# Attention scores as rounded high/low products, with the latent-head preparation and the S5 readout placed between the neighbourhood heads

## The chip, the cores and the metric

The kernel runs on one core of a Trainium2 chip, in one launch. The metric is device time in microseconds (us); the median of three runs counts. PE is the matrix engine (TensorE), PEld its weight loads, DVE the vector engine, ACT the scalar engine, POOL the GpSimd engine, and SP the engine whose queue issues most transfers.

## What is computed

Two layers over 256 latent tokens and 256 context tokens of width 1024. Each layer is a half-step SwiGLU, a token mixer and a half-step SwiGLU. The mixer has one input projection, three kinds of heads and one output projection. In layer 1 the context rows are not needed at the end, so its context queries are left out. Cut to the mixer:

```python
def token_mixers(zx, zc, need_ctx_out, ...):
    qa, ka, va, cq, ckv, kr, u = split_cols(z)       # for x (latent) and c (context) tokens
    # neighbourhood attention: 6 heads of 64, 2-D window bias, plus all context keys
    a_x = na_attention(rms_norm(qa_x), rms_norm(ka_x), va_x, rms_norm(ka_c), va_c, na_rpb)
    # latent attention: 6 heads of 64 + 32 rotary
    kb, vb = mla_keys_values(ckv, kr, ...)           # rms_norm(ckv) @ w_ukv, rms_norm over 96
    qb = mla_queries(cq, ...)                        # rms_norm(cq) @ w_uq, rms_norm over 96
    b_x = blocked_joint_attention(rope_tail(qb_x), rope_tail(kb_x), vb_x, kb_c, vb_c)
    # S5: two linear scans, readout gelu(y) @ w_glu, a * sigmoid(g)
    s_x, s_c = s5_mixer(u_x, u_c, need_ctx_out, ...)
    ox = concatenate([a_x, b_x, s_x])
    if need_ctx_out:
        oc = concatenate([attend(qa_c, ka_c, va_c), attend(qb_c, kb_c, vb_c), s_c])
    return ox, oc

def attend(q, k, v, scale):
    p = softmax(einsum('bqhd,bkhd->bhqk', q, k) * scale)
    return einsum('bhqk,bkhd->bqhd', p, v)
```

## The kernel before

All work is written out by hand; each engine runs its instructions in the order of the code, and waits are set where tiles demand them. Activations are kept with tokens or with channels on the 128 partitions, 512 tokens together.

**Products.** Weights come through `take` in pieces: SP transfers a raw piece (three buffers), ACT rounds it to its high half (L251), DVE or POOL subtracts to get the low half (L252). `mm3` (L291 to L293) makes a dense product as high by high, high by low and low by high, three products of the rounded type F32R. `acc()` gives one of four PSUM banks, `tp()` one of four others (names t and b), used for transposes and small products. The attention scores are not made in this way: they are products of F32 operands, unrounded.

**The mixer** (`mixers`) runs in this order: projection of the column groups cq, ckv, qa, ka, va. Queries and keys of the neighbourhood heads are normalised by DVE (L1227) and transposed by PE (L1117, in `transp`) into `nqT` and `nkT`. The S5 scans run in the background of these groups. Then the columns zq and zk are transposed and split into `xn` (L1246), the S5 output into `yh` (L1254), the rotary table CG is made (L1266, L1270), twelve bias transfers are issued on SP (L1299), and the **latent-head preparation** runs: up-projection of queries (four token tiles in layer 0, two in layer 1) and keys (four), each in steps head, statistics, tail. The power of the statistics is on POOL (L1134), the scaling on DVE (L1327), the rotary part on POOL (L1283 to L1285). The values are copied by ACT (L1340). The S5 **readout** (GLU: sigmoid L1375, product, split L1384) and the transposes of the latent queries (`mqT`) follow.

**Attention** is a list of jobs, per pair of heads: two tiles of latent queries ("x") for each head, and in layer 0 one of context queries ("c") for each, 36 jobs in layer 0 and 24 in layer 1. A job has scores on PE (L1458 for "x", L1467 for "c"; for neighbourhood heads the bias is added as a product with a constant flip matrix, L1463), the maximum on DVE (L1470), the exponential on ACT (L1474), the reciprocal and the scaling on DVE (L1479, L1481), four transposes on PE (L1490), copies to PT (DVE L1493, ACT L1495 and L1498) and, for each pair, the product with the values (L1510) and its split (L1513, L1514). The scores run three jobs ahead of the transposes. POOL adds the window mask to the bias (L1429). The latent keys are transposed at job 4, the output projection's first piece is split at job 6. The output projection follows.

Of the kernel before, what the change touches and what calls it, by code (L numbers as in the profile page):

```python
# [93 lines left out]
class Net:  # L94
    def __init__(self, nc, tc, I, out, es):
# [24 lines left out]
        self.rho8 = [c.tile([128, 16], F32, name=f"rho8{l}") for l in range(2)]  # L120
        self.units = []
# [203 lines left out]
    def prologue(self):  # L325
        nc, I = self.nc, self.I
        self.norm_open()
        with lines(self.tc, name="pro", bufs=1) as pp:
# [11 lines left out]
            nc.vector.memset(self.cs, 0.0)  # L340
            nc.vector.memset(self.mh, -0.5)
# [834 lines left out]
    def mixers(self, l, pu, nxt):  # L1176
# [11 lines left out]
        nq = [mp.tile([128, 3, T], F32, name=f"n{x}T") for x in "qk"]  # L1188
# [5 lines left out]
        krs = lr.tile([128, 4], F32, name="krs")  # L1194
# [21 lines left out]
        for qi, name in enumerate(("qa", "ka")):  # L1216
            tiles = al if qi else qt_
            qn = np_.tile([128, 4, 384], F32, name="qn", bufs=2)
# [33 lines left out]
        for i in range(2):  # L1252
            S.activation(yh[:, 0, i, c], yT[:, i, c], AF.Copy)
            V.tensor_tensor(yh[:, 1, i, c], yT[:, i, c], yh[:, 0, i, c].bitcast(F32), op=OP.subtract)  # L1254
        esl.close()
        mp2 = pool(es, "mixb")
        bias = mp2.tile([128, 36, 64], F32, name="bias")
        rp = I["na_rpb"]
        mq = [mp2.tile([96, 6, T], F32, name=f"m{x}T") for x in "qk"]
        mv = mp2.tile([128, 4, 6, 64], F32, name="mv")  # L1260
        knp = pool(es, "kn")
        lp = pool(esl, "mla")
        CG = lp.tile([128, 2, 4, 32], F32, name="CG")
# [9 lines left out]
        def rope(x, t, i, nh):  # L1273
# [4 lines left out]
            tm = lp.tile([128, 6, 32], F32, name="tm", bufs=2)[:, 0:nh, :]  # L1278
# [7 lines left out]

        def upproj(ct, w, nk, n, t):
            ps = [self.acc(), self.acc()] if t % 2 else [self.tp(), self.tp()]
# [6 lines left out]
        w = self.take("uq", (l,))[:, :, 0:1728].rearrange("p s (k n) -> p s k n", k=3)  # L1295
        for hf in range(2):
            for hh in range(6):
                src = bass.AP(tensor=rp.tensor, offset=rp.offset + l * 2790 + (5 - hf) * 31 - 48 + 465 * hh, ap=[[1, 64], [31, 6], [1, 64]])
                nc.sync.dma_start(bias[64 * hf:64 * hf + 64, 6 * hh:6 * hh + 6, :], src)  # L1299
# [55 lines left out]
        for i, s_ in enumerate(seq):  # L1355
# [3 lines left out]
            if i == nqs + 0:  # L1359
                pass  # L1360
# [221 lines left out]
```

## Time and profile before

| | us |
|---|---|
| median of 3 runs | 1960.72 (1958.75 to 1962.05) |
| profiled execution | 1962.65 |
| its span, first to last instruction | 1960.7 |
| block of layer 0 (column transposes to first output projection product) | 118.74 |
| block of layer 1 | 93.60 |

The table is read from the profiled execution, except for the first line. The page gives each engine's busy time and the chain of work that ended last. Windows of the trace then show which engine is busy in a stretch and at what granted clock PE ran (1.00 is 2.4 GHz, 0.50 is 1.2 GHz). A wait is named by the instruction that waits and the one that released it. PE's matmuls are pipelined, so the price of one is the distance from its start to the next start, not its own length.

### The profile page before, as it was taken

To read this page: it belongs to the slowest core of one execution; us is meant where nothing else is said; L and a number is where in the kernel's file an instruction comes from. 1 tells how busy PE (TensorE), PEld (TensorE's weight loads), DVE (VectorE), ACT (ScalarE), POOL (GpSimd) and SP (SyncE) were. 2 spreads that over 40 slices of the span, in tenths; PEclk is the share of its full clock that TensorE was granted. 3 is DMA by queue.
4 is the path that set the end of the run, shared out by engine and by line. 5 is a ranking of instruction groups with operands and counts; after the bars stand their busy time and mean duration, and the time that the engine had idled before them with its cause. 6 is when DMAs were issued, how large, how long until landed. Compare 5 with 4: busy or idle time off the path is not lost.

```text
span 1960.7 us, 28001 instructions
## 1 busy us (share of the span) xinstructions
PE 1907.6 (97%) x11345; PEld 1557.8 (79%) x11345; DVE 907.3 (46%) x1596; ACT 678.8 (35%) x1128; POOL 574.3 (29%) x661
## 2 busy tenths in 40 slices
PE   7999999999999999999999999999999988999999
PEld 4777777788896587788888877777788878579999
DVE  6453233246457835232333554423433745655555
ACT  4421222224355634222212342122223435445343
POOL 2137461124535032100101314746212545231000
PEclk9999999999999999999999999999999999799999
DMA  9656566534431024533232455656523453036563
GB/s 309 178 166 200 174 205 212 165 97 141 132 105 51 2 86 130 173 117 96 88 105 76 139 158 167 201 160 217 178 75 113 141 166 100 22 126 215 175 194 108
DMA packets 364100, 277.75 MB, mean 142 GB/s; under 512 B 29854, under 2 KB 355812, under 8 KB 363972
## 3 DMA queue, kind: packets, MB, share of 16 engines
q1 hardware_dynamic: 361008, 268.44, 44.3%
q0 software_dynamic: 1888, 7.31, 1.0%
q8 instruction: 89, 1.46, 0.3%
q10 hardware_dynamic: 1076, 0.22, 0.1%
q14 instruction: 39, 0.32, 0.0%
HBM read 263.39 MB, written 12.55 MB: 141 GB/s over the span
## 4 chain that ended last, share of the span: by engine, by line
PE 84%; DVE 6%; POOL 4%; DMA 2%; ACT 1%; SPq 1%; issue 1%; POOLq 0%; ACTq 0%; DVEq 0%
PE acc L291 24%; PE acc L292 24%; PE acc L293 23%; PE b L467 3%; PE acc L1458 2%; PE t L1490 1%; DVE xm L562 1%; PE t L1510 1%; POOL ss L1134 1%; DVE xn L572 1%; PE acc L1463 1%; POOL sqs L523 1%; PE t L1100 1%; DMA bias<-in_na_rpb 1%; DVE xn L570 1%
## 5 line engine op out<-in xcount | busy, mean ns | idle before, releaser
L291 PE MATMUL acc<-xn,spl 128*128 128x512 f32 (+1 forms) x1664 | 598.0, 359 | 8.2 <-ACT mv L1340 5.9
L292 PE MATMUL acc<-xn,spl 128*128 128x512 f32 (+1 forms) x1664 | 590.7, 355 | 1.9 <-DVE xn L396 0.2
L293 PE MATMUL acc<-xn,spl 128*128 128x512 f32 (+1 forms) x1664 | 587.3, 353 | 0.1
L252 DVE TENSOR_TENSOR spl<-raw,spl 128x1024 fp32r<-128x1024 f32 (+2 forms) x312 | 390.2, 1287 | 276.0 <-ACT spl L251 273.8
L251 ACT ACTIVATE spl<-raw 128x1024 fp32r<-128x1024 f32 (+3 forms) x344 | 324.0, 990 | 303.9 <-PE acc L293 159.6
L291 PEld LDWEIGHTS acc<-xn,spl 128*128 128x128 f32 x1664 | 315.1, 189 | 71.7 <-issue 17.8
L292 PEld LDWEIGHTS acc<-xn,spl 128*128 128x128 f32 x1664 | 315.3, 189 | 46.7 <-DVE xn L570 4.3
L672 POOL TENSOR_TENSOR hid<-hv,hid 128x512 fp32r<-128x512 f32 (+1 forms) x88 | 101.8, 1156 | 852.2 <-ACT hid L671 852.2
L293 PEld LDWEIGHTS acc<-xn,spl 128*128 128x128 f32 x1664 | 315.3, 189 | 44.7 <-DVE spl L252 0.9
L291 PE MATMUL acc<-hid,spl 128*128 128x512 f32 (+1 forms) x740 | 265.2, 358 | 0.0
L292 PE MATMUL acc<-hid,spl 128*128 128x512 f32 (+1 forms) x740 | 262.0, 354 | 0.0
L293 PE MATMUL acc<-hid,spl 128*128 128x512 f32 (+1 forms) x740 | 261.7, 354 | 0.0
L669 DVE TENSOR_TENSOR hv<-sl,acc 128x512 f32<-128x512 f32 (+1 forms) x88 | 54.7, 621 | 365.1 <-PE acc L293 353.4
L671 ACT ACTIVATE hid<-hv 128x512 fp32r<-128x512 f32 (+1 forms) x88 | 50.9, 579 | 382.0 <-DVE hv L669 382.0
L729 DVE SCALAR_TENSOR_TENSOR h<-acc,mod,h 128x256 f32<-128x256 f32 x192 | 85.0, 479 | 210.8 <-PE acc L293 210.8
L291 PEld LDWEIGHTS acc<-hid,spl 128*128 128x128 f32 x740 | 139.8, 189 | 25.2 <-issue 6.4
L293 PEld LDWEIGHTS acc<-hid,spl 128*128 128x128 f32 x740 | 139.9, 189 | 19.7
L292 PEld LDWEIGHTS acc<-hid,spl 128*128 128x128 f32 x740 | 140.0, 189 | 18.5
L252 POOL TENSOR_TENSOR spl<-raw,spl 128x768 fp32r<-128x768 f32 (+3 forms) x32 | 65.3, 2041 | 211.4 <-ACT spl L251 199.5
L291 PE MATMUL acc<-spl,xn 128*128 128x384 f32 (+1 forms) x322 | 111.5, 346 | 0.0
L292 PE MATMUL acc<-spl,xn 128*128 128x384 f32 (+1 forms) x322 | 106.9, 332 | 0.4 <-POOL spl L252 0.3
L293 PE MATMUL acc<-spl,xn 128*128 128x384 f32 (+1 forms) x322 | 106.5, 331 | 0.0
(358 smaller groups left out, 1996.8 us busy)
## 6 DMA issues: line engine op xcount, KB each, us to landing
raw<-in_ffn_w_gu SPq DMA_DIRECT2D x176, 512.0 KB
raw<-in_w_mod SPq DMA_DIRECT2D x64, 1024.0 KB
raw<-in_ffn_w_down SPq DMA_DIRECT2D x32, 1024.0 KB
raw<-in_ffn_w_down SPq DMA_DIRECT2D x16, 768.0 KB
raw<-in_w_in SPq DMA_DIRECT2D x16, 768.0 KB
pmod<-in_w_mod SPq DMA_DIRECT2D x8, 1024.0 KB
raw<-in_w_out SPq DMA_DIRECT2D x8, 1024.0 KB
cld<-CL POOLq DMA_DIRECT2D x8, 576.0 KB, 4.8
```

The lines of the kernel that those rows point to most:

```text
L251: nc.scalar.activation(s[:, 0, a:b], raw[:, a:b], AF.Copy)
L252: (nc.gpsimd if mix and b == n else nc.vector).tensor_tensor(s[:, 1, a:b], raw[:, a:b], s[:, 0, a:b].bitcast(F32), op=OP.subtract)
L291: mm(out, sl[0], sr[0], start=start, stop=False)
L292: mm(out, sl[0], sr[1], start=False, stop=False)
L293: mm(out, sl[1], sr[0], start=False, stop=stop)
L467: nc.tensor.matmul(p[32 * j:32 * j + 32, 0:256], self.cs[:, k, 6 - 2 * w:38 - 2 * w], raw[:, k, :], start=(a == 0 and w == 0), stop=(a == ...
L523: nc.gpsimd.tensor_tensor(self.sq_sum[:, c], self.sq_sum[:, c], s[:, c], op=OP.add)
L669: nc.vector.tensor_tensor(hv[:, c], sl[:, c], pu[:, c], op=OP.mult)
L671: nc.scalar.activation(hd[:, 0, c], hv[:, c], AF.Copy)
L672: nc.gpsimd.tensor_tensor(hd[:, 1, c], hv[:, c], hd[:, 0, c].bitcast(F32), op=OP.subtract)
L729: self.nc.vector.scalar_tensor_tensor(self.h[:, n, c], ps[:, c], self.mod[l][:, gate, n, s:s + 1], self.h[:, n, c], op0=OP.mult, op1=OP.add)
L1458: mm(s, q[:, 256 + 128 * t:384 + 128 * t], k, start=True, stop=h >= 6)
```

## The change

Scores and bias are made of rounded products. Queries and keys are kept as a high and a low F32R half (`qz`, zero-padded to 128 rows so that a head's query meets a pair's keys, and `keyt`); a score is three products (L1522, context L1530), the bias two more (L1525) with its halves made on POOL (L1457, L1459, L1460). The transposes of `qa` and `ka` leave the groups; `keys` (per pair) and `queries` (per head) make them within attention, ACT the high half and DVE the low one. Latent-head preparation and readout become a generator, `latent()`, of which one piece runs after each job, so they lie among the neighbourhood heads. Latent heads are transposed by `latent_head`, one head each, two heads ahead. The scaling of the first "x" tile and of context tiles goes from DVE to POOL (L1544). The PT copy of odd context heads goes from ACT to DVE. Heads now run one after another and not in pairs of jobs. Bias transfers go out two heads at a time. The readout takes channel slots 0 and 1 and attention's outputs slots 2 to 7.

```diff
+        biases = [bias(h) for h in range(2)]
+        kr = mp.tile([128, 4, 32], F32, name="kr")
+        krs = mp.tile([128, 4], F32, name="krs")
...
-            def tr(j, qi=qi, tiles=tiles, qn=qn):
-                self.transp(nq[qi][:, j, 128 * tiles[0]:], lambda t: qn[:, t, 128 * j:128 * j + 128], 128, tiles, self.kg[l][:, 0:1] if qi else None)
-
-            self.q += [None, None, None] + [(lambda j=j, tr=tr: tr(j)) for j in range(3)]
...
-            ps = [self.acc(), self.acc()] if t % 2 else [self.tp(), self.tp()]
+            ps = [self.tp(), self.tp()]
...
+        def glu(n, wg):
+            pg = {}
+            for m in (2 + n, n):
+                pg[m] = self.tp()
+                for k in range(2):
+                    self.mm3(pg[m][:, c], (wg[:, 0, k, m * 128:m * 128 + 128], wg[:, 1, k, m * 128:m * 128 + 128]), (yh[:, 0, k, c], yh[:, 1, k, c]), k == 0, k == 1)
+            eg = mp2.tile([128, 576], F32, name="sq6")[:, 0:T]
+            S.activation(eg[:, c], pg[2 + n][:, c], AF.Sigmoid, bias=self.smT[l][:, 98 + n:99 + n])
+            V.scalar_tensor_tensor(eg[:, c], pg[n][:, c], self.smT[l][:, 96 + n:97 + n], eg[:, c], op0=OP.add, op1=OP.mult)
+            S.activation(xn[:, 0, n, c], eg[:, c], AF.Copy)
+            (V, P)[n].tensor_tensor(xn[:, 1, n, c], eg[:, c], xn[:, 0, n, c].bitcast(F32), op=OP.subtract)
+        def latent():
+            w = self.take("uq", (l,))[:, :, 0:1728].rearrange("p s (k n) -> p s k n", k=3)
+            for t in (2, 3, 0, 1):
+                rope(kr[:, t].unsqueeze(1), t, 1, 1)
+            seq = [(qhead, qstat, qtail, t) for t in [2, 3] + qt_[:-2]]
+            nqs = len(seq)
+            seq += [(khead, kstat, ktail, t) for t in al]
+            for i in range(len(seq) + 2):
+                if i == nqs:
+                    w = self.take("ukv", (l,), True)[:, :, 0:1536].rearrange("p s (k n) -> p s k n", k=2)
+                if i < len(seq):
+                    seq[i][0](seq[i][3], w)
+                for j in (1, 2):
+                    if 0 <= i - j < len(seq):
+                        seq[i - j][j](seq[i - j][3])
+                yield
+            wg = self.take("glu", (l,), False)[:, :, 0:1024].rearrange("p s (k n) -> p s k n", k=2)
+            for n in range(2):
+                glu(n, wg)
+                yield
+            self.ahead()
+        self.attention(l, need, qt_, qk, nv, qs, kn, mv, biases, bias, xn, mp2, latent())
...
+        def keys(p):
+            g = self.kg[l][:, 0:1]
+            kt = keyt[p % 2]
+            c = cols(lambda t: qk[1][:, t, 128 * p:128 * p + 128], al, 128)
+            S.activation(kt[:, 0], c, AF.Copy, scale=g)
+            V.scalar_tensor_tensor(kt[:, 1], c, g, kt[:, 0].bitcast(F32), op0=OP.mult, op1=OP.subtract)
+            for h in (2 * p, 2 * p + 1):
+                stacks[h] = [None, kt, None]
+        def queries(h):
+            r = slice(64 * (h % 2), 64 * (h % 2) + 64)
+            q = qz[h % 2]
+            c = cols(lambda t: qk[0][:, t, 128 * (h // 2):128 * (h // 2) + 128], qt_, 128)
+            S.activation(q[r, 0, t0:], c[r, 0:nq], AF.Copy)
+            V.tensor_tensor(q[r, 1, t0:], c[r, 0:nq], q[r, 0, t0:].bitcast(F32), op=OP.subtract)
+            b = biases.pop(0)
+            P.tensor_tensor(b, b, bc(self.k[:, K_WIN:K_WIN + 64].unsqueeze(1), [128, 6, 64]), op=OP.add)
+            bb = [ap.tile([128, 6, 64], F32R, name=f"bb{i}", bufs=2) for i in range(2)]
+            P.tensor_copy(bb[0], b)
+            P.tensor_tensor(bb[1], b, bb[0].bitcast(F32), op=OP.subtract)
+            if h < 4:
+                biases.append(bias(h + 2))
+            stacks[h][0] = q
...
+        def latent_head(h):
+            j, g = h - 6, self.kg[l][0:96, 1:2]
+            q, kt = qz[h % 2], keyt[1 - h % 2]
+            c = cols(lambda t: qs[t][:, j, :], qt_, 96)
+            S.activation(q[0:96, 0, t0:], c[0:96, 0:nq], AF.Copy)
+            V.tensor_tensor(q[0:96, 1, t0:], c[0:96, 0:nq], q[0:96, 0, t0:].bitcast(F32), op=OP.subtract)
+            c = cols(lambda t: kn[t][:, j, :], al, 96)
+            S.activation(kt[0:96, 0], c[0:96], AF.Copy, scale=g)
+            V.scalar_tensor_tensor(kt[0:96, 1], c[0:96], g, kt[0:96, 0].bitcast(F32), op0=OP.mult, op1=OP.subtract)
+            stacks[h] = q, kt, None
...
+        def after(i):
+            p, n = i // (2 * each), i % (2 * each)
+            if p < 2:
+                if n == 2 * each - 2:
+                    keys(p + 1)
+                    queries(2 * p + 2)
+                elif n == 2 * each - 1:
+                    queries(2 * p + 3)
+            elif p == 2:
+                if n == 2 * each - 2:
+                    for _ in latent:
+                        pass
+                    latent_head(6)
+                elif n == 2 * each - 1:
+                    latent_head(7)
+            elif n % each == each - 1 and i // each + 2 < 12:
+                latent_head(i // each + 2)
...
+            terms = [(q[r, i], ks[r, j]) for i, j in ((0, 0), (0, 1), (1, 0))]
+            if kind == "x":
+                for i, (q, k) in enumerate(terms):
+                    mm(s, q[:, 256 + 128 * t:384 + 128 * t], k, start=i == 0, stop=h >= 6 and i == 2)
                 if h < 6:
                     for i in range(2):
+                        mm(s[:, 256:512], self.flip, bb[i][:, 64 * (2 - 2 * t):64 * (6 - 2 * t)], start=False, stop=i == 1)
+                nb, n = 1, 512
...
+                for b in range(2):
+                    for i, (q, k) in enumerate(terms):
+                        mm(s[:, 256 * b:256 * b + 256], q[:, 128 * b:128 * b + 128], k[:, 0:256], start=i == 0, stop=i == 2)
...
+                (P if j[2] == 0 else V).tensor_scalar(e[:, i * n:i * n + n], e[:, i * n:i * n + n], su[:, i:i + 1], None, op0=OP.mult)
...
+            if t or (kind == "c" and h % 2):
+                V.tensor_copy(d, v)
+            else:
+                S.activation(d, v, AF.Copy)
...
+        for i in range(len(jobs) + LAG):
+            if i < len(jobs):
+                scores(jobs[i])
+                after(i)
+            if 0 < i <= len(jobs):
+                scale(jobs[i - 1])
+            if i >= LAG:
+                transposes(jobs[i - LAG])
+            for a in old.pop(0):
                 pv(*a)
+            old.append(pend[:])
+            pend.clear()
+            next(latent, None)
```

PE, layer 0, at the start of attention, before: after the column transposes (zq, zk) the first latent up-projection follows (t and b are PSUM banks, spl a weight piece).

```order
L1117 MATMUL t<-k,zq 128x128 x8
L1117 MATMUL b<-k,zq 128x128 x4
L1117 MATMUL t<-k,zk 128x128 x8
L291 MATMUL t<-spl,xn 128x288
L292 MATMUL t<-spl,xn 128x288
L293 MATMUL t<-spl,xn 128x288
L291 MATMUL t<-spl,xn 128x288
```

The same place of the changed kernel: transposes of a pair's keys (nk) and of two heads' queries (nq), the first score with its bias, then the first up-projection.

```order
L1119 MATMUL b<-k,zq 128x128 x4
L1119 MATMUL t<-k,zq 128x128 x8
L1119 MATMUL t<-k,zk 128x128 x4
L1119 MATMUL b<-k,zk 128x128 x4
L1436 MATMUL t<-k,nk 128x128 x4
L1436 MATMUL t<-k,nq 128x128 x8
L1522 MATMUL acc<-kt,qz_4762 128x512 x3
L1525 MATMUL acc<-bb_4781,flip 128x256
L1525 MATMUL acc<-bb_4782,flip 128x256
L292 MATMUL b<-spl,xn 128x288
```

So a score now stands between the transposes and the first up-projection.

POOL, layer 0, during the latent-head preparation, before: powers (L1134) and rotary parts (L1283 to L1285) of the latent queries (qn), with a window add (L1429).

```order
L1134 TENSOR_TENSOR ss_4886<-ss_4886,mh 128x6
L1134 TENSOR_TENSOR ss_4915<-ss_4915,mh 128x6
L1283 TENSOR_TENSOR tm<-qn,CG 128x6x8 x4
L1284 TENSOR_TENSOR qn<-qn,CG 128x6x32
L1285 TENSOR_TENSOR qn<-qn,tm 128x6x32
L1134 TENSOR_TENSOR ss_4952<-ss_4952,mh 128x6
L1283 TENSOR_TENSOR tm<-qn,CG 128x6x8 x4
L1284 TENSOR_TENSOR qn<-qn,CG 128x6x32
L1285 TENSOR_TENSOR qn<-qn,tm 128x6x32
L1134 TENSOR_TENSOR ss_4992<-ss_4992,mh 128x6
```

The same place of the changed kernel, with the scaling of tiles (L1544) and the bias splits (L1457 to L1460).

```order
L1544 TENSOR_SCALAR e<-e,su 128x512
L1136 TENSOR_TENSOR ss_4905<-ss_4905,mh 128x6
L1136 TENSOR_TENSOR ss_4949<-ss_4949,mh 128x6
L1290 TENSOR_TENSOR tm<-qs,CG 128x6x8 x4
L1291 TENSOR_TENSOR qs<-qs,CG 128x6x32
L1292 TENSOR_TENSOR qs<-qs,tm 128x6x32
L1544 TENSOR_SCALAR e<-e,su 128x256 x2
L1136 TENSOR_TENSOR ss_5007<-ss_5007,mh 128x6
L1290 TENSOR_TENSOR tm<-qs,CG 128x6x8 x4
L1291 TENSOR_TENSOR qs<-qs,CG 128x6x32
L1292 TENSOR_TENSOR qs<-qs,tm 128x6x32
L1457 TENSOR_TENSOR bias<-bias,k 128x384
```

Tile scalings and bias splits have come between the powers and the rotary parts, in one queue.

## Rows read from the trace of the kernel before

**Rows 1.** The profile page: shares of the chain that ended last, by engine

```profile
PE 84%; DVE 6%; POOL 4%; DMA 2%; ACT 1%; SPq 1%; issue 1%; POOLq 0%; ACTq 0%; DVEq 0%
```

**Rows 2.** Stretches: window, length, busy (count) by engine, granted clock, DMA share, GB/s

```profile
574.66:693.40 118.74, 112.89 (x621) 76.44 (x619) 92.60 (x214) 71.09 (x180) 33.91 (x45) 0.97 0.16 45
1639.60:1733.20 93.60, 86.22 (x427) 54.36 (x425) 67.35 (x150) 47.70 (x110) 29.33 (x43) 0.89 0.20 57
583.00:610.20 27.20, 23.79 (x129) 21.21 (x127) 19.72 (x47) 12.83 (x29) 24.71 (x38) 0.87 0.34 114
654.40:687.20 32.80, 32.80 (x190) 20.51 (x189) 28.07 (x72) 22.39 (x66) 0.00 (x0) 1.00 0.00 1
539.54:546.37 6.83, 6.31 (x21) 5.82 (x22) 2.23 (x3) 2.79 (x5) 1.87 (x1) 0.50 0.54 149
600.98:607.81 6.83, 5.80 (x15) 4.49 (x16) 4.60 (x12) 4.79 (x10) 5.28 (x6) 0.50 0.00 0
1665.94:1686.42 20.48, 19.55 (x38) 8.74 (x39) 10.83 (x26) 6.85 (x15) 8.95 (x11) 0.50 0.00 1
```

**Rows 3.** PE's waits by the window 505:693.4, then 1605:1733.2: total, times, longest

```profile
PE acc L291 <- ACT mv L1340: 3.4, 1, 3.4
PE t L1117 <- DVE qn L1227: 2.7, 1, 2.7
...
PE t L1117 <- DVE mqT L1125: 3.3, 1, 3.3
```

**Rows 4.** Timeline of PE in layer 0: start, length, operation, count

```profile
577.49 0.40 PE L291 MATMUL t<-spl,xn 128*128 128x288 f32 x1
...
638.17 1.13 PE L1467 MATMUL acc<-nkT,nqT 64*128 64x256 f32 x4
639.23 0.66 PE L1490 MATMUL t<-k,e 128*128 128x128 f32 x4
639.82 1.12 PE L1458 MATMUL acc<-nkT,nqT 64*128 64x512 f32 x2
640.87 0.70 PE L1463 MATMUL acc<-bias,k 128*128 128x256 f32 x2
641.41 0.60 PE L1490 MATMUL t<-k,e 128*128 128x128 f32 x4
...
665.03 0.60 PE L1490 MATMUL t<-k,e 128*128 128x128 f32 x4
665.47 1.02 PE L1458 MATMUL acc<-mkT,mqT 96*128 96x512 f32 x2
666.34 0.60 PE L1490 MATMUL t<-k,e 128*128 128x128 f32 x4
...
693.97 0.40 PE L293 MATMUL acc<-xn,spl 128*128 128x512 f32 x1
694.20 0.40 PE L291 MATMUL acc<-xn,spl 128*128 128x512 f32 x1
```

**Rows 5.** Groups by line on POOL, 505:693.4: count, busy us, mean ns, idle before

```profile
L1134 POOL TENSOR_TENSOR ss<-ss,mh 128x6 f32<-128x6 f32 (+1 forms) x17 | 22.7, 1338 | 19.6 <-DVE ss L1133 19.6
...
L1429 POOL TENSOR_TENSOR bias<-bias,k 128x384 f32<-128x384 f32 x6 | 5.3, 897 | 0.0
...
L1384 POOL TENSOR_TENSOR xn<-zq,xn 128x512 fp32r<-128x512 f32 x1 | 1.3, 1267 | 3.5 <-ACT xn L1383 3.5
```

**Rows 6.** Timelines of DVE and POOL, layer 0: start, length, operation, count

```profile
579.32 1.28 DVE L1254 TENSOR_TENSOR xn<-yT,xn 128x512 fp32r<-128x512 f32 x2
...
630.42 2.46 POOL L252 TENSOR_TENSOR spl<-raw,spl 128x1024 fp32r<-128x1024 f32 x1 [13.08 <-ACT spl L251]
...
631.36 1.81 DVE L1481 TENSOR_SCALAR e<-e,su 128x512 f32<-128x512 f32 x1
...
633.88 0.49 DVE L1481 TENSOR_SCALAR e<-e,su 128x512 f32<-128x512 f32 x1
```

**Rows 7.** Timeline of ACT at the layer-0 GLU

```profile
605.23 1.28 ACT L1375 ACT_TABLE_LOAD   x1
```

More of the change, by code (lines that the diff above doesn't have):

```diff
@@ L1217, in mixers @@
             tiles = al if qi else qt_
[L1218 removed]
+            qn = qk[qi]
             def norm(t, qn=qn):
@@ L1293, in upproj @@
             return ps
[L1295 to L1299, printed above, removed]
-        qs, kn = {}, {}
-        for t in (2, 3, 0, 1):
-            rope(zk[:, t, 256:288].unsqueeze(1), t, 1, 1)
-        new = lambda: lp.tile([128, 6, 96], F32, name="qn", bufs=4)
-        ss = {}
         def stat(key, sq, extra=None):
-            ss[key] = lp.tile([128, 6], F32, name="ss6", bufs=4)
+            ss[key] = mp2.tile([128, 6], F32, name="ss6", bufs=4)
             V.tensor_reduce(ss[key], sq, axis=AX, op=OP.add)
@@ new lines, in attention @@
+        keyt = [ap.tile([128, 2, T], F32R, name="kt"), ox[:, :, 7]]
+        qz = [ap.tile([128, 2, T], F32R, name=f"qz{i}") for i in range(2)]
+        for i in range(2):
+            r = slice(64 - 64 * i, 128 - 64 * i)
+            P.memset(qz[i][r].bitcast(F32), 0.0)
+        def after(i):
[15 more added lines that the diff above has]
+                latent_head(i // each + 2)
@@ new lines, in scale, with transposes @@
+        def scale(j):
+            e, su, nb, n = st[j]
+            V.reciprocal(su[:, 0:nb], su[:, 0:nb])
+            for i in range(nb):
+                (P if j[2] == 0 else V).tensor_scalar(e[:, i * n:i * n + n], e[:, i * n:i * n + n], su[:, i:i + 1], None, op0=OP.mult)
+        def transposes(j):
+            kind, h, t = j
+            e = st.pop(j)[0]
+            if (kind, h) not in PT:
+                PT[kind, h] = ap.tile([128, 4 if kind == "x" else 2, 256], F32, name=f"PT{kind}", bufs=3)
+            p = self.tp()
+            for i in range(4):
+                nc.tensor.transpose(p[:, 128 * i:128 * i + 128], e[:, 128 * i:128 * i + 128], self.ident)
+            if kind == "x":
+                d, v = PT[kind, h][:, :, 128 * t:128 * t + 128], p.rearrange("p (k q) -> p k q", k=4)
+            else:
+                d, v = PT[kind, h].rearrange("p k (t q) -> p t k q", t=2), p.rearrange("p (t k q) -> p t k q", t=2, k=2)
+            if t or (kind == "c" and h % 2):
+                V.tensor_copy(d, v)
+            else:
+                S.activation(d, v, AF.Copy)
+            if h % 2 and (t or kind == "c"):
+                pend.append((kind, h))
@@ new lines, in pv @@
+        def pv(kind, h):
+            o = self.tp()
+            nk = 4 if kind == "x" else 2
+            pts = [PT.pop((kind, h - 1)), PT.pop((kind, h))]
+            for k in range(nk):
+                for i in range(2):
+                    mm(o[64 * i:64 * i + 64, 0:256], value(h - 1 + i)(k), pts[i][:, k, :], start=(k == 0), stop=(k == nk - 1))
+            c = slice(256, 512) if kind == "x" else slice(0, 256)
+            f = h // 2 + 2
+            S.activation(ox[:, 0, f, c], o[:, 0:256], AF.Copy)
+            V.tensor_tensor(ox[:, 1, f, c], o[:, 0:256], ox[:, 0, f, c].bitcast(F32), op=OP.subtract)
@@ L1538, in run @@
+        for a in old[0] + old[1]:
+            pv(*a)
     def run(self):
```

226 lines of the change are left out of this document (69 added, 157 removed).

## The prediction

> **What bounds the kernel now.** I read the chain of waits first: 84% of the path to the end is matrix work on PE, 6% DVE, 4% POOL [rows 1]. So a change pays if PE gets less to do or waits less, and costs if another engine takes its place. The change touches one stretch in each layer, from the column transposes of the latent-rank inputs to the first output-projection product, and the column groups just ahead of it. The table by stretches [rows 2] gives for the layer-0 block 118.74 us with PE busy 112.89, DVE 92.60, ACT 71.09 and POOL 33.91, and for the layer-1 block 93.60 with PE 86.22. PE is the limit of both on average. It is not so everywhere: in the latent-head preparation (27.20 us) POOL is busy 24.71 and PE 23.79, while through the latent heads (32.80 us) PE is busy all the time and POOL does nothing. The same table shows three stretches in which PE's granted clock is 0.50, half of 2.4 GHz: 6.83, 6.83 and 20.48 us. Each comes right behind one of PE's longest waits, of 2.7, 3.4 and 3.3 us [rows 3]. A stretch at 0.50 does its PE work in twice the time, so it loses half of its busy PE time: 6.31/2 = 3.2 in the groups, 5.80/2 = 2.9 in the layer-0 block, 19.55/2 = 9.8 in the layer-1 block [rows 2].
>
> **Score products.** Prices are taken from start to start in the timeline of PE [rows 4]. A neighbourhood tile over the latent queries takes 640.87 − 639.82 = 1.05 for the score and 641.41 − 640.87 = .54 for the bias, 1.59 together; a context tile of the same heads 639.23 − 638.17 = 1.06; a latent tile 666.34 − 665.47 = .87. A rounded product of 512 columns, as the kernel uses everywhere else, takes 694.20 − 693.97 = .23, and I take half of it, .115, for 256 columns. Three of 512 are .69; with two bias products of 256 a neighbourhood tile comes to .92. A context tile, six products of 256, comes to .69. That these tiles keep this pace with their own weight loads is an estimate; its two ends are all of the gain below and none.
> Layer 0 has 12 neighbourhood tiles (12 × .67 = 8.0), 12 latent tiles (12 × .18 = 2.2), 6 context tiles of neighbourhood heads (6 × .37 = 2.2) and 6 of latent heads, for which I take the latent row's .87 (6 × .18 = 1.1): 13.5. Layer 1 has the first two: 10.2.
> The Trainium skill, page "FP8 and Floating Point Precision", section "TensorE Precision Notes", says that true FP32 takes four passes through the array. By it a tile of 512 columns takes 4 × .23 = .92; the latent row (.87) agrees, the neighbourhood row (1.05) does not, and the gain would be about 24 × .13 = 3 us smaller.
>
> **Transposes.** Four of them cost 665.47 − 665.03 = .44 [rows 4]. The groups lose six sets in layer 0 (2.6) and, with half the queries, the worth of 4.5 sets in layer 1 (2.0). Attention gains three sets for keys and six for queries, since a pair's query columns are now transposed for each head: 9 × .44 = 4.0, in layer 1 3 × .44 + 6 × .22 = 2.6. The latent heads keep their twelve sets and only take them later.
>
> **Groups.** With the transposes leaves their wait of 2.7 for the normalised queries, and with it, I expect, the half-speed stretch behind it (3.2): −2.6 − 2.7 − 3.2 = **−8.5** in layer 0. If another wait keeps the clock low the two last terms shrink; the least is −2.6. Layer 1 shows no such wait: **−2.0**.
>
> **Layer-0 block without new waits.** PE's busy time less the half-speed loss is 112.89 − 2.9 = 110.0; − 13.5 + 4.0 gives 100.5. To that come waits, which are the uncertain part.
> (a) The start. The first score now needs the low halves of keys and of two heads' queries, which DVE makes after the column work. DVE's two subtractions for the readout start at 579.32 and take 1.28 [rows 6], so it is free at 580.6; short products of table CG (an estimate, .3 if nothing disturbs them) and three subtractions at .64 each, half of those 1.28, end at 582.8. PE has done its transposes earlier: they now begin where the first up-projection product began, at 577.5 [rows 4], and three sets are 1.3, so 578.8. The wait is 4.0, between 2 and 6. It is as long as those that precede the three slow stretches, so I add the 2.9 that the slow stretch of this block loses now: 7.
> (b) The stretch in which preparation and neighbourhood heads share the engines, ten jobs. PE has about 33 there: the up-projections (4 × 18 products of 288 columns and 4 × 12 of 384, at .23 × columns / 512, are 17.6) and ten jobs at some 1.6 (a tile of .9, a set of transposes, and values now and then, which start late). POOL has its 24.71 [rows 2], less two window adds (L1429, .90 each [rows 5]), plus seven scaled tiles and two heads' bias splits. No row shows a scaling or a cast on POOL: between .5, DVE's price for the same tile [rows 6], and 1.27, POOL's own price for a subtraction of 512 [rows 5]; I take 1.15, nearer to POOL's row. A head's split is add, cast, subtract at .90, .75 and .90. So 24.7 − 1.8 + 8.1 + 5.1 = 36. POOL passes PE by 3, and its queue is in order: a scale waits behind a power (1.34 [rows 5]) that waits for DVE's sum, and behind the scale wait the transposes of that tile on PE; DVE's normalisation of the latent queries (L1327) in turn waits for the power. I take 8, between 3 and 20.
> (c) Pair boundaries, where the next pair's keys and queries are made one or two jobs ahead, and three more table loads on ACT for sigmoid and exponential between jobs, 1.28 each [rows 7]: 4, between 1 and 10. (d) The end: the last context tile's scaling is on POOL before its transposes: 2, between 0 and 4.
> 100.5 + 7 + 8 + 4 + 2 = 121.5 against 118.74: **+2.8**.
>
> **Layer-1 block.** 86.22 − 9.8 = 76.4; − 10.2 + 2.6 = 68.8. Waits: start 6.5, preparation 7 (jobs are fewer per head, so less PE work covers the same POOL chain), boundaries 3, end 1.5: 86.8 against 93.60: **−6.8**. The reason is the 20.48 us at half speed behind a wait for the first latent queries' transposes, which the new order spreads out.
>
> **Costed at nothing.** The bias transfers now stand in pairs in SP's queue and each waits until POOL has used the buffer two heads earlier; behind it stand weight transfers three units ahead, and the DMA engines are busy 0.16 to 0.20 in these blocks [rows 2]. The zeroing of the query buffers and a copy of the rotary columns on POOL lie where POOL is idle. Moving half the scales relieves DVE. If this cover were gone, a late weight piece would show as an output projection that waits, a few us.
>
> **Sum.** −8.5 + 2.8 − 2.0 − 6.8 = −14.5. The profiled execution took 1962.65, some 2 more than the median of 1960.72; the difference is applied to both: 1948.2 and **1946.2**.
>
> **Rivals.**
> 1. The waits are covered: in each block only the low ends remain, 6 in layer 0 (106.5, −12.2) and 5 in layer 1 (73.8, −19.8). With −10.5 in the groups −42.5, so 1918. For it: PE has work from two sources there, and the lag of three jobs between score and transposes is some 5 us at 1.6 a job. Against it: POOL's sum above PE's.
> 2. Slower: POOL and DVE stop each other. While POOL's split of 2.46 ran, DVE's scaling of 512 columns took 1.81 in place of .49 [rows 6]. Each layer moves 12 tiles or more to POOL and leaves 12 scalings on DVE, now beside a busy POOL even in the latent heads, where POOL was idle before. If all 24 that stay on DVE meet one and the path goes through them, 24 × 1.32 = 31.7; the time is 1946.2 + 31.7 = 1978. From 11 such meetings on the path the change no longer pays. Against it: the latent heads' DVE work falls, and a tile has three jobs before PE needs it.
> The Trainium skill, page "SBUF — State Buffer", section "Who interferes with whom", says that DVE and GpSimd share a port pair, that the first to issue holds it for the whole instruction, and that the other is blocked fully. It speaks against giving POOL the scales; the .49 that became 1.81 agrees.
> 3. The products do not run at the dense pace: no gain from them, +23.7, so 1970.
>
> **Chances.** Forecast .58 (1932 to 1958), rival 1 .18, rival 2 .19, rival 3 .05. The range reaches from just above the low rival to where half of the slow ones lie: 1920 to 1970. A measurement of this kernel can tell about 0.2% (4 us) from no change. Faster by more: .72, from rival 1 and most of the forecast; within: .09; slower: .19.
>
> **What would show it.** Right: tiles of score and bias at .9 in PE's timeline; no wait of PE in the query and key groups; a first score that waits for DVE's L1455; PE waits in the preparation that name POOL's L1544 or L1136; the layer-1 block about 7 shorter, the layer-0 block within a few us of its length. Wrong: scores that cost over 1.2 (rival 3); DVE scalings over 1 us in the latent heads and PE waiting for them (rival 2); preparation without PE waits (rival 1). The step on which most hangs is (b), and whether half speed follows the new waits.

## The result: slower by 2.3%, and the profile after

The changed kernel takes 2007.23 us (2004.01 to 2008.59, four runs) against 1961.38 before; the ratio is 1.0233, with a 95% interval of 1.0216 to 1.0251. The forecast was 1946.2 within 1920 to 1970, so sign and range are both missed.

The page of the changed kernel gives its span, busy time by engine and PE's granted clock in 40 slices:

```profile
span 2006.8 us, 28327 instructions
...
PE 1904.8 (95%) x11435; PEld 1582.0 (79%) x11435; DVE 914.7 (46%) x1585; ACT 689.8 (34%) x1146; POOL 656.2 (33%) x739
...
PEclk9999999999989899999999999999999988999999
```

PE's busy time is about what it was (1907.6 us before), while the span has grown by 46.1. By the start of the column transposes and of the first output-projection product in PE's timelines, the 46.1 lie so: 1.0 before the layer-0 block, 31.1 in it (149.83 against 118.74), 3.1 between the blocks, 10.9 in the layer-1 block (104.05 against 93.14, from the transposes' own start at 1640.04). After it the two kernels are equal to 0.1 us. The windows of these blocks, and of three stretches of the first, have the columns of [rows 2]:

```profile
575.65:725.48 149.83, 117.38 (x705) 93.50 (x703) 91.18 (x199) 79.84 (x192) 85.12 (x95) 0.89 0.15 38
1675.22:1779.28 104.06, 78.06 (x472) 61.62 (x470) 68.24 (x153) 56.99 (x128) 58.63 (x69) 0.93 0.22 54
583.00:630.00 47.00, 39.10 (x217) 35.78 (x219) 30.57 (x64) 21.82 (x55) 39.17 (x53) 0.85 0.36 82
630.00:672.00 42.00, 29.82 (x177) 22.02 (x174) 21.55 (x45) 23.95 (x49) 22.54 (x22) 0.88 0.12 41
672.00:719.00 47.00, 39.46 (x250) 29.85 (x249) 30.01 (x67) 26.42 (x73) 20.43 (x19) 0.89 0.00 1
```

Length less busy time is PE's idle time. In layer 0 it was 118.74 − 112.89 = 5.9 us and is 149.83 − 117.38 = 32.4; in layer 1 it was 7.4 and is 26.0. A mean clock of 0.89 means that some 2 × .11 × 149.83 = 33 us ran at half speed (7 before). Taking half of PE's busy time in such stretches off, read slice by slice from the windows, its work at full speed is 102.8 in layer 0 (110.0 before) and 71.7 in layer 1 (76.0). So PE has less to do, as intended, and the time is lost to waits and to the half speed that follows them: in layer 0 +26.6 idle, +11.6 half speed, −7.2 work; in layer 1 +18.6, −3.4 and −4.3.

PE's longest waits from the column groups to the end of the layer-0 block, in the columns of [rows 3], are not one wait but many:

```profile
PE t L1553 <- DVE e L1544: 7.3, 4, 2.6
PE t L1553 <- POOL e L1544: 6.6, 6, 2.9
PE acc L293 <- DVE spl L253: 6.0, 2, 3.7
PE b L1553 <- POOL e L1544: 3.6, 1, 3.6
PE t L1553 <- ACT PTc L1561: 3.0, 2, 2.3
PE t L292 <- DVE xn L1445: 2.9, 1, 2.9
PE acc L1522 <- ACT qz L1454: 2.6, 1, 2.6
PE t L292 <- DVE kt L1445: 2.5, 1, 2.5
```

L1553 are the transposes of the exponentials; they wait for the scaling (L1544) on DVE and on POOL and for copies of earlier tiles. L292 and t are an up-projection and a readout product that wait for the PSUM bank in which a key transpose still stands, until DVE has taken its low half (L1445). The wait of 6.0 for a weight piece is new too: it lies in the groups (3.7 and 2.2) and replaces the 2.7 of [rows 3].

One of the waits followed back, in the latent heads, in the timelines of DVE, ACT and PE (start, length, operation):

```profile
687.13 0.68 DVE L1533 TENSOR_REDUCE m<-acc 128x2 f32<-128x512 f32 x1
689.38 0.69 DVE L1472 TENSOR_TENSOR qz<-t,qz 96x512 fp32r<-96x512 f32 x1 [1.56 <-ACT qz L1471]
689.99 0.74 DVE L1475 SCALAR_TENSOR_TENSOR kt<-t,kg,kt 96x512 fp32r<-96x512 f32 x1
690.64 0.15 DVE L1542 RECIPROCAL su<-su 128x1 f32<-128x1 f32 x1
690.83 0.49 DVE L1544 TENSOR_SCALAR e<-e,su 128x512 f32<-128x512 f32 x1
```

```profile
687.85 0.47 ACT L1537 ACTIVATE e<-acc,m 128x256 f32<-128x256 f32 x1 [1.09 <-DVE m L1533]
...
688.76 0.58 ACT L1471 ACTIVATE qz<-t 96x512 fp32r<-96x512 f32 x1
```

```profile
688.30 0.94 PE L1522 MATMUL acc<-xn,qz 96*128 96x512 f32 x3
691.47 0.30 PE L1553 MATMUL t<-k,e 128*128 128x128 f32 x1 [2.22 <-DVE e L1544]
```

DVE has taken the maximum of a context tile by 687.8. Its next instruction in the queue is the low half of a later head's queries, which needs ACT's high half, and that stands on ACT behind the two exponentials of the same context tile. DVE idles 1.56, makes two low halves, and only then scales a tile of an earlier job, for which PE waits 2.22 us in all. DVE's 1.56 return at each of the later latent heads; PE waits behind every second of them: 1.96, 2.22 and 2.57.

### The profile page after: what moved, and what is told of

It is laid out like the page before. It is cut to its first block, busy times and chain, and to the rows that moved or that the text cites. A ratio compares the mean times of both kernels' runs of the same rounds, so it can differ in the third digit from the quotient of the medians.

```text
span 2006.8 us, 28327 instructions
## 1 busy us (share of the span) xinstructions
PE 1904.8 (95%) x11435; PEld 1582.0 (79%) x11435; DVE 914.7 (46%) x1585; ACT 689.8 (34%) x1146; POOL 656.2 (33%) x739
## 5 line engine op out<-in xcount | busy, mean ns | idle before, releaser
L292 PE MATMUL acc<-xn,spl 128*128 128x512 f32 (+1 forms) x1648 | 591.3, 359 | 2.3 <-DVE xn L571 1.2
L293 PE MATMUL acc<-xn,spl 128*128 128x512 f32 (+1 forms) x1648 | 584.6, 355 | 1.9 <-DVE xn L398 0.2
L294 PE MATMUL acc<-xn,spl 128*128 128x512 f32 (+1 forms) x1648 | 580.9, 353 | 0.2 <-DVE spl L253 0.2
L253 DVE TENSOR_TENSOR spl<-raw,spl 128x1024 fp32r<-128x1024 f32 (+2 forms) x312 | 398.2, 1313 | 278.6 <-ACT spl L252 276.8
L292 PEld LDWEIGHTS acc<-xn,spl 128*128 128x128 f32 x1648 | 311.7, 189 | 64.2 <-issue 17.8
L293 PEld LDWEIGHTS acc<-xn,spl 128*128 128x128 f32 x1648 | 311.8, 189 | 46.9 <-DVE xn L572 4.6
L294 PEld LDWEIGHTS acc<-xn,spl 128*128 128x128 f32 x1648 | 311.7, 189 | 44.1 <-DVE spl L253 0.9
L292 PE MATMUL acc<-hid,spl 128*128 128x512 f32 (+1 forms) x740 | 265.2, 358 | 0.0
L292 PEld LDWEIGHTS acc<-hid,spl 128*128 128x128 f32 x740 | 139.8, 189 | 25.2 <-issue 6.4
L293 PEld LDWEIGHTS acc<-hid,spl 128*128 128x128 f32 x740 | 140.0, 189 | 18.6
L293 PE MATMUL acc<-spl,xn 128*128 128x384 f32 (+1 forms) x288 | 98.0, 340 | 8.5 <-DVE spl L253 8.2
L292 PE MATMUL acc<-spl,xn 128*128 128x384 f32 (+1 forms) x288 | 101.2, 351 | 0.0
L294 PE MATMUL acc<-spl,xn 128*128 128x384 f32 (+1 forms) x288 | 97.5, 338 | 0.0
L669 ACT ACTIVATE sl<-acc 128x512 f32<-128x512 f32 (+1 forms) x88 | 47.7, 541 | 133.8 <-PE acc L294 127.5
```

The lines of the kernel that those rows point to most:

```text
L253: (nc.gpsimd if mix and b == n else nc.vector).tensor_tensor(s[:, 1, a:b], raw[:, a:b], s[:, 0, a:b].bitcast(F32), op=OP.subtract)
L292: mm(out, sl[0], sr[0], start=start, stop=False)
L293: mm(out, sl[0], sr[1], start=False, stop=False)
L294: mm(out, sl[1], sr[0], start=False, stop=stop)
L669: nc.scalar.activation(sl[:, c], pg[:, c], AF.Silu)
```

## The experiments

All ratios are to the kernel before, timed in the same series.

**Order and place of the scaling.** Run 1 moves the scaling ahead of the preparation of later heads:

```diff
             if i < len(jobs):
                 scores(jobs[i])
-                after(i)
             if 0 < i <= len(jobs):
                 scale(jobs[i - 1])
+            if i < len(jobs):
+                after(i)
```

> One thing is reordered against the changed kernel: in each job the scaling of the job before (reciprocal, multiply) is written ahead of the preparation of a later head's keys and queries, not behind it. Theory A (the low halves of later keys and queries wait on DVE for ACT behind the job's own exponential, and hold up the scaling behind them): the waits of PE's transposes for the DVE-scaled tile (7.3 us in layer 0, 3.7 to 4.1 us waits in layer 1) go and with them the half-speed stretches that follow; about 18 us less, 1989. Theory B (the tiles are late because POOL takes 1.56 to 1.83 us for a scaling): 0 to 4 us less, 2003 to 2007.

Measured: 1999.71, ratio 1.0194 (1.0174 to 1.0214), some 7.5 us less than the change, between the two theories. The waits for DVE-scaled tiles went (7.3 to .6), but those for POOL-scaled ones stayed:

```profile
PE t L1553 <- POOL e L1544: 9.0, 11, 3.0
PE b L1553 <- POOL e L1544: 3.6, 1, 3.6
```

Run 2 puts all scalings on DVE:

```diff
-                (P if j[2] == 0 else V).tensor_scalar(e[:, i * n:i * n + n], ...)
+                V.tensor_scalar(e[:, i * n:i * n + n], ...)
```

> All scalings on DVE, as in the kernel before; nothing else is changed. Theory A: the queue order stays, the DVE queue only gets longer; 0 to 6 us less, 2001 to 2007. Theory B: PE's waits for POOL-scaled tiles (10.0 and 6.8 us) go, with some half-speed time; about 18 us less, 1989. If POOL and DVE had stopped each other at the shared port, more still.

Measured: 2009.96, 1.0251 (1.0234 to 1.0268): no gain. PE's waits only changed their name:

```profile
PE t L1553 <- DVE e L1544: 9.4, 6, 2.3
...
PE b L1553 <- DVE e L1544: 2.9, 1, 2.9
```

Run 3 has both edits.

> Scaling first and all of it on DVE. If A and B both hold and add up: about 35 us less, 1972. If either alone is the cause, no better than the better of the two single runs, about 1989.

Measured: 1999.17, 1.0189 (1.0170 to 1.0208), as run 1. Theory B has fallen: POOL's long scalings are not the cause, though PE waits by that name. Theory A holds for a sixth of the loss.

Run 4 runs the preparation whole ahead of attention (`for _ in latent: pass` ahead of `keys(0)`).

> The latent-head preparation and the readout run whole ahead of attention, as in the kernel before; scores, scalings and order of the attention jobs stay those of the changed kernel. Theory C (the loss lies in the interleaving, POOL's and ACT's queues shared by two kinds of work): about 15 us less, 1992. Theories A and B: the waits of the jobs stay and the preparation has no cover, 0 to 8 us more, 2007 to 2015.

Measured: 2004.70, 1.0224 (1.0202 to 1.0245), not to be told from the change. As a net account, putting it in pieces neither costs nor gains as long as the rest stands, and theory C falls. Under that net lie two sums: waits behind the pieces go (they are followed back in the next section), and PE idles 42.09 − 30.05 = 12.0 us ahead of the first score, in a preparation that nothing covers:

```profile
575.77:617.86 42.09, 30.05 (x178) 25.96 (x176) 31.84 (x66) 22.30 (x45) 28.23 (x41) 0.92 0.08 26
```

PE's idle time in the whole layer-0 block (length less busy time) hardly moves through these four runs: 30.3, 28.7, 30.1 and 30.1 us, against 32.4 in the change.

**Depth, low halves, banks, products.** These four stand on top of run 1. Run 5 has one job more between a score and its transposes:

```diff
-        LAG = 3
+        LAG = 4
```

> On top of scaling first: scores run four jobs ahead of the transposes instead of three (one more buffer of e, m and su; one PTc buffer less to make room). Theory F (the distance between score and transposes is too short now that a score takes PE .7 to .9 us and the way over DVE, ACT and POOL is longer): PE's waits for scaled tiles, 12.6 us in layer 0 and some 10 in layer 1, go mostly, with half-speed time behind them: about 18 us less than 1999.7, 1982. Theory G (the PSUM banks of the column transposes are held by the chain ACT high half, DVE low half, and all else in the same ring waits): 0 to 3 us less, 1997 to 2000.

Measured: 1993.12, 1.0168 (1.0150 to 1.0186), 5 to 7 us less than run 1: between the two theories.

Run 6 leaves the low halves of queries and keys out:

```diff
-            V.tensor_tensor(q[r, 1, t0:], c[r, 0:nq], q[r, 0, t0:].bitcast(F32), op=OP.subtract)
...
-            terms = [(q[r, i], ks[r, j]) for i, j in ((0, 0), (0, 1), (1, 0))]
+            terms = [(q[r, 0], ks[r, 0]) for _ in range(3)]
```

> On top of scaling first: the low halves of queries and keys are not made (DVE's subtractions are left out) and the products read the high half in their place, so that PE's work is the same; the result is not the attention's. Theory G: the waits for banks held by the subtractions go (about 13 us in layer 0, as much in both layers with the half-speed time): about 20 us less, 1980. Theory F: DVE has 24 x .7 = 17 us less to do in layer 0, but the way of a tile is the same: 0 to 5 us less, 1995 to 2000.

Measured: 1986.16, 1.0122 (1.0106 to 1.0138), 14 us less than run 1 with the same products on PE, between the theories and nearer to G. The waits for L1445 are gone from the list. Run 6 takes away three things at once: the time of the subtractions on DVE, their place in its queue, and their hold on a bank that others wait for.

Run 7 gives the column transposes another ring of banks (`self.acc()` for `self.tp()` in `cols`).

> On top of scaling first: the column transposes of queries and keys in attention take their PSUM bank from the ring of the scores instead of the ring shared by the other transposes, the value products and the up-projections. Theory G, if the shared ring is the point: waits of L292, L1553 and L1571 for DVE's subtractions go, about 10 to 15 us less, 1985 to 1990. Theory F: the same or, since scores now wait for those banks, up to 5 us more, 1999 to 2005.

Measured: 1995.65, 1.0180 (1.0156 to 1.0204), 4 us below run 1 but within its interval: no clear gain, which speaks against the bank as the larger part of the 14. Run 3 has 14 us more on DVE in the layer-0 block than run 1 (105.43 busy against 91.24) and takes the same time, which speaks against DVE's time as such. That leaves the place of the low halves in DVE's queue; this is argued and not shown by a run of its own.

Run 8 keeps the order but goes back to one F32 product per tile, and so makes no low halves and no bias splits either:

```diff
-            terms = [(q[r, i], ks[r, j]) for i, j in ((0, 0), (0, 1), (1, 0))]
+            terms = [(q[r, 0].bitcast(F32), ks[r, 0].bitcast(F32))]
...
-                        mm(s[:, 256:512], self.flip, bb[i][:, 64 * (2 - 2 * t):64 * (6 - 2 * t)], ...)
+                    mm(s[:, 256:512], self.k[:, K_FLIP:K_FLIP + 128], bb[0][...], start=False, stop=True)
```

> On top of scaling first: the new order with the old products: one F32 product per score tile and one for the bias, no low halves and no bias split (the operands are rounded high halves read as F32, so the result is that of rounded operands). PE's work rises by about 20 to 24 us over both layers, DVE's and POOL's falls. If the new products and their halves are what costs, it falls towards the kernel before plus the extra transposes, about 1970. If the new order alone costs (preparation in pieces, heads one after another), it stays at 1995 to 2005.

Measured: 1980.61, 1.0096 (1.0081 to 1.0111). With more work on PE it is 19 us faster than run 1, and still 19 slower than before, between the two expectations. Along this path the 46 us are 7.5 for the place of the scaling, 19 for the rounded products with their halves and bias splits, and 19 for the order. Its two blocks, columns as in [rows 2]:

```profile
573.43:709.73 136.30, 116.65 (x657) 83.42 (x656) 78.39 (x178) 79.67 (x192) 75.96 (x83) 0.95 0.16 41
1659.36:1752.34 92.98, 79.80 (x447) 55.99 (x445) 55.87 (x132) 56.97 (x128) 49.32 (x57) 0.96 0.24 60
```

The layer-1 block is as long as before; the layer-0 block is 17.6 longer. Its idle time is 136.30 − 116.65 = 19.7 against 5.9 before, which is 13.8 of the 17.6.

**What is left of the order, with F32 products.** Run 10 takes run 8 and the preparation ahead, run 11 takes run 8 and scalings on DVE, run 13 both, run 14 both and LAG 4.

> The run with F32 scores in the new order, with the latent-head preparation and readout whole ahead of attention, as in the kernel before. If the 17.5 us that this order still costs in layer 0 come from preparation in pieces: about 15 us less, 1966. If they come from the order of jobs and the column transposes within attention: 1980 or, the preparation being uncovered, up to 10 us more.

> The run with F32 scores in the new order, with all scalings on DVE, which has no low halves to make there. If the waits for POOL-scaled tiles (9.6 us in layer 0) are what is left: about 12 us less with the half-speed time, 1969. If those waits only pass to another step of the tile's way: 1978 to 1982.

> F32 scores in the new order, with both the preparation ahead of attention and all scalings on DVE. Left of the change are the order of jobs, head by head, and the column transposes within attention. If the two shares add up: 1980.6 - 3.9 - 5.2 = 1971.5, and what is left (10 us) is the price of job order and transposes. If each only showed a part of the same wait and the two together free it: 1962 to 1966.

> The same with scores four jobs ahead. If what is left is the distance between a score and its transposes (heads one after another bring the context tile, which needs two exponentials and two scalings, into every third place): 5 to 8 us less, 1964 to 1966. If it is the transposes and their copies in the queues: 1970 to 1972.

Measured: 1976.69, 1.0072 (1.0058 to 1.0085); 1975.41, 1.0069 (1.0056 to 1.0083); 1973.84, 1.0065 (1.0050 to 1.0080); 1971.21, 1.0045 (1.0029 to 1.0062). Each alone gives some 4 to 5 us, with an interval that still meets that of run 8, and both together hardly more (6), so the two do not add up in full. With LAG 4 (six runs, 1966.76 to 1974.96), 10 of the 19 us are gone and 9 remain. In run 13 the longest waits of PE are at the head of attention (L1436 are the column transposes, L1516 the first score, L1453 ACT's copy of its queries, L1360 and L1361 the readout, whose banks the transposes wait for):

```profile
PE t L1436 <- ACT sq L1360: 3.7, 2, 2.7
PE acc L1516 <- ACT qz L1453: 3.3, 1, 3.3
PE t L1436 <- DVE sq L1361: 1.6, 1, 1.6
```

Its window up to just before the first score (620.92), in the columns of [rows 2]:

```profile
578.85:620.00 41.15, 30.17 (x177) 26.10 (x175) 30.97 (x65) 21.39 (x43) 27.30 (x41) 0.93 0.08 26
```

PE idles 11.9 us up to that score and 1.5 in the rest of the block; the kernel before idles 5.9 in all of it. So in layer 0 what is left lies in the uncovered preparation and between it and the first score, and not in the order of the jobs behind it. What the up-projections lose by their smaller ring of banks (`ps` in the diff) was not tried by itself.

**All mends with the rounded products.** Run 12 has run 1, LAG 4 and the other banks; run 15 adds preparation ahead and scaling on DVE.

> The changed kernel with three mends together: scaling first, four jobs of distance, column transposes in the banks of the scores. Alone they gave 7.5, 6.6 and 4.1 us. If they are separate waits: about 1989. If they are the same waits under other names: 1991 to 1993, as the best of them.

> The changed kernel, rounded products, with all mends at once: preparation ahead of attention, scaling first and on DVE, four jobs of distance, columns in the banks of the scores. If the products and low halves cost by DVE's time, which is now the fullest beside PE: 1985 to 1990, no better than three mends. If the mends add up: about 1978.

Measured: 1989.80, 1.0143 (1.0127 to 1.0158), and 1993.77, 1.0166 (1.0149 to 1.0183), the second above both of its expectations. No arrangement tried with low halves comes within 1.4% of the kernel before.

**A part of the change that pays.** Run 8 showed something else: an F32 score of a neighbourhood head took .86 us and not 1.05, and its zero-padded queries have 128 rows where the kernel before multiplies 64. Run 9 puts only this into the kernel before (the other rows are zeroed once by POOL, and one PTc buffer less makes room):

```diff
-                    return nq[0][r, h // 2, :], nq[1][r, h // 2, :], ...
+                    return qz[h % 2], nq[1][:, h // 2, :], ...
...
+            def pad(h):
+                r = slice(64 * (h % 2), 64 * (h % 2) + 64)
+                P.tensor_copy(qz[h % 2][r, t0:], nq[0][r, h // 2, t0:])
```

> The kernel before with one thing of the change: the neighbourhood heads' queries are copied by POOL, two heads ahead, into two buffers of 128 rows whose other 64 rows are zero, so that F32 score products run over 128 rows instead of 64. If the 1.05 us of a score before came from the 64-row operands (the F32 run in the new order showed .86, and .43 for the bias instead of .54): 12 x .2 + 6 x .2 + 12 x .1 = 4.8 us less in layer 0, 3.6 in layer 1, 1953. If the price comes from elsewhere, or POOL's copies hold up DVE's scalings: 1960 to 1965.

Measured: 1957.11, 0.9971 (0.9960 to 0.9982), between the two expectations. The layer-1 block is 3.7 shorter, though its first score waits 5.7 us for POOL; the layer-0 block is not shorter, and its first score waits longer:

```profile
PE acc L1468 <- POOL qz L1446: 6.3, 1, 6.3
```

Run 16 lets the first pair read its 64 rows as before and pads from the second on (`if h < 2:` with the old operands).

> The kernel before with zero-padded F32 queries as in the padded run, but from the second pair of heads on; the first pair reads its 64 rows as before, so that no score waits for POOL's first copies. If the padded operands are the gain and the waits of 6.3 and 5.7 us were its price: two thirds of the work saved (6 us) without the waits, 1953 to 1955, 3 us below the padded run. If PE's shorter scores are given back to waits for tiles of the same jobs: 1957 to 1960.

Measured: 1955.12, 0.9965 (0.9953 to 0.9977), 7 us below the kernel before and the fastest kernel run here, though not clearly below run 9. Its layer-0 block, now 3.2 shorter than before, in the columns of [rows 2], and a score with its bias in PE's timeline:

```profile
574.69:690.21 115.52, 109.37 (x621) 77.15 (x620) 92.81 (x214) 70.86 (x180) 37.50 (x51) 0.97 0.16 46
```

```profile
638.38 1.02 PE L1471 MATMUL acc<-nkT,qz 128*128 128x512 f32 x2
639.24 0.59 PE L1476 MATMUL acc<-bias,k 128*128 128x256 f32 x2
639.67 0.60 PE L1503 MATMUL t<-k,e 128*128 128x128 f32 x4
```

From start to start the score is .86 and the bias .43, against 1.05 and .54 in [rows 4], with PE idle 6.2 us as before.

## Why the prediction was wrong

Between 1946 and 2007 lie 61 us. By stretch: the layer-0 block was forecast +2.8 and came out +31.1; the layer-1 block −6.8 and +10.9; the groups of layer 0 −8.5 and +1.0; the layer-1 groups −2.0, where all between the blocks came out +3.1.

**Products: right in kind, a little small.** PE's work at full speed is 102.8 and 71.7 where the sum had 100.5 and 68.8. From start to start a neighbourhood tile takes .69 + .24 (forecast .92) and a context tile .71 (forecast .69), at best:

```profile
597.34 0.86 PE L1522 MATMUL acc<-kt,qz 128*128 128x512 f32 x3
598.03 0.40 PE L1525 MATMUL acc<-bb,flip 128*128 128x256 f32 x2
598.27 0.60 PE L1553 MATMUL t<-k,e 128*128 128x128 f32 x4
...
642.56 0.87 PE L1530 MATMUL acc<-xn,qz 128*128 128x256 f32 x6
643.27 0.60 PE L1436 MATMUL t<-k,nq 128*128 128x128 f32 x4
```

The .69 holds for a score behind a dense product. Behind transposes or values it took .77 to .81, in latent heads (687.15 to 687.95) as in neighbourhood heads (649.02 to 649.79); why was not tried. Rival 3 is refuted. The part of the gain that came from padded operands (.19 a score and .11 a bias) was put down to rounding; run 16 shows it to be had without.

**Groups: wrong.** The transposes' own −2.6 came true. But the prediction also took out a wait of 2.7 and its half-speed stretch and did not say what is late next. The transposes had stood in front of products that need DVE's low half of the next weight piece, and DVE makes it behind the same normalisation: PE now waits for that (3.7 and 2.2, the 6.0 above), and half speed stays at 6.8 us in the groups, as before.

**Start (a) and end (d): about right; preparation (b): the size by luck.** The first score waited 2.6, for ACT's high half L1454 and not for DVE's L1455, and its bias .9 more (forecast 4.0), with half speed behind it. The last transposes waited 2.0 (forecast 2). From 583 to 630 PE idles 47.00 − 39.10 = 7.9 (forecast 8), but the forecast had POOL's full queue as the reason, and only 1.4 of it names POOL's scaling L1544. Of the rest .9 is the bias again, 2.9 is an up-projection that waits for the bank of the next pair's keys, which is a pair boundary, and 2.6 are ACT's copies L1561. In layer 1 the first score waited 2.1 for POOL's zeroing of the query buffers, which was costed at nothing.

**Boundaries (c) and latent heads: this step failed.** It had 4 us for the pair boundaries and three table loads, and costed the latent heads' transposes at nothing since they "only take them later". In the windows above PE idles 12.2 us from 630 to 672 and 7.5 from 672 to 719, nearly 20 in place of 4, and 8 more go to half speed there.

In the latent heads (672 to 719) 6.7 of the 7.5 are the three waits for a tile scaled on DVE. What moved was not only PE's transposes but a chain on three engines, ACT's high half and DVE's low half, in front of the softmax of earlier jobs. Run 6 prices the low halves at some 14 us over both layers; run 1 prices the place of the scaling behind them at 7.5.

From 630 to 672 the low halves are the smaller part: 2.5 is the readout product that waits for the bank of a key transpose, and 2.5 are ACT's copies. The other 7.0 are tiles that are scaled late, since a piece of `latent()` stands ahead of their scaling in the queues of DVE and POOL: first the second half of the readout (L1363), whose sigmoid waits for a table load (1.28), then the split of a weight piece (L253), which waits for its high half on ACT. Timelines of POOL and PE:

```profile
652.02 1.26 POOL L1363 TENSOR_TENSOR xn<-sq,xn 128x512 fp32r<-128x512 f32 x1 [7.47 <-DVE su L1542]
653.26 1.83 POOL L1544 TENSOR_SCALAR e<-e,su 128x256 f32<-128x256 f32 x2
654.24 0.44 PE L1553 MATMUL t<-k,e 128*128 128x128 f32 x2 [2.90 <-POOL e L1544]
...
656.49 2.43 POOL L253 TENSOR_TENSOR spl<-raw,spl 128x1024 fp32r<-128x1024 f32 x1 [1.41 <-ACT spl L252]
658.91 3.53 POOL L1544 TENSOR_SCALAR e<-e,su 128x512 f32<-128x512 f32 x3
660.69 1.11 PE L1553 MATMUL b<-k,e 128*128 128x128 f32 x4 [3.65 <-POOL e L1544]
```

In run 4, where these pieces run ahead of attention, no wait for a tile scaled on POOL is longer than 1.0; the price there is the uncovered preparation. The cover that was trusted (three jobs between a score and its transposes) was too short for this way: run 5 got 5 to 7 us back with a fourth. That it shrank because the jobs became shorter is argued, not tried.

**Half speed: forecast only behind the start.** The windows show the clock at 0.85 to 0.89 in each of the three stretches; in layer 0 this cost 14.5 us in place of the 2.9 entered. In layer 1 it cost some 6.4, less than the 9.8 of before, but not nothing.

**Rival 2: the right sign, mostly for a wrong reason.** In the blocks POOL's work hardly lengthened DVE's scalings. The twelve that stayed on DVE took .49 on average beside a POOL busy for 85 us, as before with POOL idle; the groups by line on the two engines in the layer-0 block:

```profile
L1544 DVE TENSOR_SCALAR e<-e,su 128x512 f32<-128x512 f32 x12 | 5.9, 490 | 0.4
...
L1544 POOL TENSOR_SCALAR e<-e,su 128x256 f32<-128x256 f32 (+1 forms) x36 | 41.5, 1163 | 36.9 <-DVE su L1542 36.8
```

By the two timelines, as far as POOL's rough spans tell, five of the twelve ran beside a POOL instruction for .4 to .5 us, and took .49 to .53 all the same. Run 2, without scalings on POOL, was no faster. POOL's idle time in the second row (36.9 us before its scalings, for DVE's reciprocal) says the same: POOL was mostly not the bound there, it waited too.

The blocking that the Trainium skill describes ("SBUF — State Buffer", section "Who interferes with whom": the engine that comes second waits out the whole instruction of the first) shows in [rows 6], not in these five, and once more in the column groups, where it is part of PE's wait of 3.7. Timelines of DVE and POOL, and the product that waits:

```profile
535.18 0.56 DVE L1241 TENSOR_TENSOR nq<-nq,ss 128x384 f32<-128x384 f32 x1 [1.50 <-POOL ss L1136]
...
537.85 3.89 POOL L253 TENSOR_TENSOR spl<-raw,spl 128x768 fp32r<-128x768 f32 x2
537.91 2.16 DVE L1241 TENSOR_TENSOR nq<-nq,ss 128x384 f32<-128x384 f32 x1 [1.50 <-POOL ss L1136]
540.00 3.42 DVE L253 TENSOR_TENSOR spl<-raw,spl 128x768 fp32r<-128x768 f32 x2
...
542.61 0.45 PE L293 MATMUL acc<-spl,xn 128*128 128x384 f32 x1 [3.73 <-DVE spl L253]
```

The same normalisation took .56 alone and 2.16 beside POOL's split of a weight piece. The kernel before has this too (2.15 at 537.79), so it is not new with the change, but it is part of why the groups still wait.

What stays open is how the last 9 us of the order with F32 products divide between the two layers and the smaller ring of banks.

## What to carry to other kernels

Before work is taken off the bounding engine in a pipelined loop, lay out one job's whole way over all engines and ask what distance of jobs covers it; with shorter jobs on the bounding engine the same distance covers less time. When a step is moved into such a loop, each of its instructions takes a place in an in-order queue: write work on which the loop waits ahead of work that itself waits for another engine. When PE's waits change their name with each mend and the sum stays, count idle time per stretch and not per name.

## What was not expected of the hardware

An F32 product of 512 columns with operands of 64 rows took 1.05 us [rows 4], and .86 with the queries padded with zeros to 128 rows (runs 8, 9 and 16); context tiles took 1.06 and .86. With the latent heads' 96 rows it took .86 to .87 all along. On POOL a scaling of 512 columns took 1.56 us, above the 1.15 entered, and a cast of 384 columns .50, below the .75 entered.
